# A pooling branch's projection as Strassen products over output pairs, feature halves and token halves

## The chip, the cores and the metric

The kernel runs on one core of one Trainium2 chip. The metric is the device time of one execution in microseconds, as a median of several runs. All matrix products are float32 products made of three matmuls on float32r pieces (high part times high part, high times low, low times high), so one logical 128x128 by 128x512 product is three TensorE instructions.

## The reference, cut to what matters

One layer of a hybrid decoder trunk, with 1024 tokens of 1024 channels. The part that the change touches is the product `y_a W_a` in the middle of this:

```python
h = rms_norm(x, norm_mix)
u_pool, q, k, v, g_a, g_b = split(h @ w_in)
y_a = pool_mixer(u_pool, w_pool, pool_scale)      # 1024 tokens x 512 channels
y_b = stick_breaking_attention(q, k, v)           # 8 heads of 64
merged = sigmoid(g_a) * (y_a @ w_branch_a) + sigmoid(g_b) * (y_b @ w_branch_b)
x = x + merged @ w_out                            # then SwiGLU, embedding gate, norm
```

`w_branch_a` is 512 x 1024.

## The kernel before

Everything is kept transposed: a tile has 128 channels on the partitions and 512 tokens (half of the sequence, `HALF`) on the free axis. Stages that follow one another and matter here:

- The stage of `u`, then four projections to q and k (`to_qk`, 0, 4, 1, 5) with the four pooling groups (`pool_mix`) between them. `pool_mix` makes window sums on VectorE in tiles `win`, splits them into `plh` and `pll`, multiplies by `w_pool` (two halves of three matmuls) and evicts with `split_gain` straight into float32r pairs `yah`, `yal` of 128 x 1024 (one ScalarE and one VectorE instruction for each half).
- The projection to v: 8 banks of PSUM `vb`, 192 matmuls with the weights moving. Bank `tt` holds 128 tokens; it is evicted in four instructions, ScalarE and VectorE in turn (`split_gain` on even and odd heads), into a tile `vs` of 4 KB a partition, of which there are two, and then written to `d_v` in HBM. Token tiles 0, 2, 4, 6 use the first `vs`, and 1, 3, 5, 7 the second. A `vs` is free again when its write has landed.
- The projection of the pooling branch, which is what changes: for each of eight output blocks `m` a weight load of 128 x 512 (`w_a[m]`), its split into `whi` and `wlo`, and for each half of the tokens a bank of PSUM that gathers four channel blocks of three matmuls each (`project`, lines 84 to 86), 192 matmuls in all. ScalarE copies the bank into a tile `ev` or `sg` (two of each), and that is written to `d_t[m]` in HBM. Behind the weight of `m == 2` the loads of head 0 of the attention (`head_loads(0)`, tiles `hq`, `hkh`, `hkl`, `hv`) are issued.
- The attention, with an order of TensorE's instructions that is written out by hand. The remaining projections to q and k and the two gates run in it as fillers; `gate_a` reads `d_t` back.

Outside the parts written out by hand a planner lays the instructions of each engine in an order: of those that it takes to be ready, the one earliest in the program. The order in the queue of an engine is then fixed, and an engine waits at the front of its queue.

SBUF is handed out as two stacks of pools, one growing from the left and one (`side="right"`) from the right. A pool that is opened after another has been closed lies over the closed one's bytes, and a tile there waits for the old tiles with which it shares bytes, and for those alone (`reuse_waits="tile"`). In a pool, the tiles of one name lie side by side, the names in order of their first use, and the first tile of a name takes the lowest place. In KB a partition, from where `up` begins: `up` has `u0` to `u3` (16); `ab` has `wpraw`, `wph`, `wpl`, `evh`, `evl` (2 each), `win`, `plh`, `pll` and `vs` (two of 4 each). When these are closed, `hlp` (two each of `hq`, `hkh`, `hkl`, `hv`, 4 each) and then the pool of the attention (`beta`, `fail` two of 4 each, `evh`, `evl` two of 2 each, then `ath` of 2 each) begin at the same byte. `wp` holds two each of `wraw`, `whi`, `wlo` (4 each).

Of the kernel before, what the change touches and what calls it, by code (L numbers as in the profile page):

```python
# [25 lines left out]
HALF = 512  # L26
# [18 lines left out]
def hybrid_block(ctx, tc, xT, pT, gains, pscale, w_u, w_qk, w_v, w_ga, w_gb, w_pool, w_a, w_b,  # L45
                 w_out, w_gate, w_up, w_down, w_pg, w_pp, out):
    nc = tc.nc

    def pool(name, bufs=1, **kw):
        return tc.tile_pool(name=name, bufs=bufs, reuse_waits="tile", **kw)  # L50
# [11 lines left out]
    ps_sb = const.tile([P, 4], F32, name="ps_sb")  # L62
# [5 lines left out]
    def hs(h):  # L68
        return slice(h * HALF, (h + 1) * HALF)


    def weight(src, cols):
        raw = wp.tile([P, D], F32, name="wraw")
        hi = wp.tile([P, D], F32R, name="whi")
        lo = wp.tile([P, D], F32R, name="wlo")
        nc.sync.dma_start(raw[:, :cols], src)
        for c in range(0, cols, HALF):
            cs = slice(c, c + HALF)
            split(hi[:, cs], lo[:, cs], raw[:, cs])
        return hi, lo  # L80

    def mm3(ps, w, x, first, last, onto=False):

        nc.tensor.matmul(ps, w[0], x[0], start=first, stop=False, skip_group_check=onto)  # L84
        nc.tensor.matmul(ps, w[0], x[1], start=False, stop=False, skip_group_check=onto)  # L85
        nc.tensor.matmul(ps, w[1], x[0], start=False, stop=last, skip_group_check=onto)  # L86

    def col(w, k):
        return w[0][:, k * P:(k + 1) * P], w[1][:, k * P:(k + 1) * P]

    def part(x, sl):
        return x[0][:, sl], x[1][:, sl]

    def steps(ps, w, x, sl, n=KT):
        for k in range(n):
            mm3(ps, col(w, k), part(x[k], sl), k == 0, k == n - 1)
            yield

    def project(ps, w, x, sl, n=KT):
        for _ in steps(ps, w, x, sl, n):  # L100
            pass

    def split(hi, lo, src, eng=None):
# [42 lines left out]
    def new_pair():  # L146
        return xhp.tile([P, S], F32R, name="xs"), xhp.tile([P, S], F32R, name="xs")
# [10 lines left out]
    d_t = [scr(f"d_t{i}", [P, S]) for i in range(KT)]  # L158
# [11 lines left out]
    wp = ph1.enter_context(pool("wp", 2))  # L170
    tmp = ph1.enter_context(pool("tmp", 2))
    xhx = ph1.enter_context(ExitStack())
    xhp = xhx.enter_context(pool("xhp", 2 * KT))
    ab = ph1.enter_context(ExitStack())
    up = ab.enter_context(pool("up"))
    ps8x = ph1.enter_context(ExitStack())
    ps8 = ps8x.enter_context(pool("ps8", 8, space=PSUM))
# [5 lines left out]
    with pool("start") as st:  # L183
        acc = st.tile([P, S], F32, name="acc")
        ps = ps8.tile([P, HALF], F32, name="mm")
# [3 lines left out]
        for k in range(KT):  # L189
            xt = st.tile([P, S], F32, name="xt", bufs=3)  # L190
            w = st.tile([P, HALF], F32, name="wraw", bufs=3)
            wh = st.tile([P, HALF], F32R, name=f"wuh{k}")
            wl = st.tile([P, HALF], F32R, name=f"wul{k}")
            pair = new_pair()
# [66 lines left out]
            move(dst[0, :, hs(h)], hi)  # L261
            move(dst[1, :, hs(h)], lo)

    yap = ExitStack()
    yp = yap.enter_context(pool("yap", side="right"))
    abp = ab.enter_context(pool("ab"))

    ya = []
    raw = abp.tile([P, 4 * P], F32, name="wpraw")
    wph = abp.tile([P, 4 * P], F32R, name="wph")  # L270
    wpl = abp.tile([P, 4 * P], F32R, name="wpl")
    nc.sync.dma_start(raw, w_pool)
    split(wph, wpl, raw)

    def pool_mix(g, w):
        cur, step = u[g], 1
        while step < w:
            nxt = abp.tile([P, S], F32, name="win", bufs=2)
            nc.vector.tensor_add(nxt[:, :S - step], cur[:, :S - step], cur[:, step:])
            nc.vector.tensor_copy(nxt[:, S - step:], cur[:, S - step:])  # L280
            cur, step = nxt, step * 2
        po = abp.tile([P, S], F32, name="win", bufs=2)
        n = S - w + 1
        nc.vector.scalar_tensor_tensor(po[:, :n], cur[:, :n], 1.0 / w, u[g][:, :n], ALU.mult, ALU.subtract)
        nc.vector.tensor_mul(po[:, n:], cur[:, n:], rcnt[:, 16 - w:15])
        nc.vector.tensor_sub(po[:, n:], po[:, n:], u[g][:, n:])
        pl = (abp.tile([P, S], F32R, name="plh", bufs=2), abp.tile([P, S], F32R, name="pll", bufs=2))
        split(*pl, po)
        y = (yp.tile([P, S], F32R, name=f"yah{g}"), yp.tile([P, S], F32R, name=f"yal{g}"))
        for h in range(2):  # L290
            ps = ps8.tile([P, HALF], F32, name="mm")
            mm3(ps, col((wph, wpl), g), part(pl, hs(h)), True, True)
            split_gain(*part(y, hs(h)), ps, ps_sb[:, g:g + 1])
        ya.append(y)

    def run(x):
        for _ in x:
            pass
# [6 lines left out]
    pool_mix(2, WINDOWS[2])  # L305
    run(to_qk(abp, ps8, 5))
    pool_mix(3, WINDOWS[3])


    vb = [ps8.tile([P, HALF], F32, name="mm") for _ in range(KT)]  # L310
    for j in range(4):
        w = weight(w_v[j], D)
        for e in range(2):
            k = 2 * j + e
# [54 lines left out]
        return q, kh, kl, v  # L369

    loads = {}
    for m in range(KT):
        w = weight(w_a[m], 4 * P)
        if m == 2:
            loads[0] = head_loads(0)
        for h in range(2):
            ps = ps8.tile([P, HALF], F32, name="mm")
            project(ps, w, ya, hs(h), 4)
            t = tmp.tile([P, HALF], F32, name=("ev", "sg")[h])
            nc.scalar.copy(t, ps)  # L380
            nc.sync.dma_start(d_t[m][:, hs(h)], t)
    ps8x.close()
    yap.close()

# [5 lines left out]
    with att, pool("att", 2) as ap, ExitStack() as pss:  # L390
# [111 lines left out]
        with tc.manual_schedule(engines={nc.tensor.engine}):  # L502
            for s in range(len(slots) + LAG + AVLAG):
                if s < len(slots):
                    h, qt = slots[s]
# [20 lines left out]
    def bank():  # L526
        return psp.tile([P, HALF], F32, name="mm")
# [3 lines left out]
    for i, t in enumerate(yb):  # L531
        pair = ybsp.tile([P, S], F32R, name=f"ybh{i}"), ybsp.tile([P, S], F32R, name=f"ybl{i}")
# [44 lines left out]
    for m in range(KT):  # L577
        w = weight(w_b[m], 4 * P)
        for h in range(2):
            sg = rp.tile([P, HALF], F32, name="rg")  # L580
# [3 lines left out]
            ps = bank()  # L584
# [32 lines left out]
    for m in range(KT):  # L617
        w = pieces(w_out[m])
        nc.sync.dma_start(x2[m][:, hs(0)], xT[m][:, hs(0)])
        ps = bank()  # L620
# [7 lines left out]
    for m in range(4):  # L628
        w = pieces(w_out[m])
        nc.sync.dma_start(x2[m][:, hs(1)], xT[m][:, hs(1)])  # L630
        ps = bank()
        whole(ps, w, mg, hs(1))
        if m == 3:
            w = pieces(w_out[4])
# [150 lines left out]
    for m in range(4, KT):  # L785
        ps = bank()
# [3 lines left out]
        if m < KT - 1:  # L790
            w = [halves(r) for r in raws]
# [21 lines left out]
    y = const.tile([P, KT], F32, name="nrm_y", bufs=2)[:, :4]  # L813
# [24 lines left out]
    y12 = normed(0, 1)  # L838
    for i in range(4):
        y22 = normed(i + 4, 1)  # L840
        nc.scalar.copy(b22[i][0], y22)
        nc.gpsimd.tensor_sub(unsplit[i][1], y22, y12)
        y11 = normed(i, 0)
        if i < 3:
            embed(i + 1, 0)
        nxt = normed(i + 1, 1) if i < 3 else None
# [25 lines left out]
        y12 = nxt  # L872
# [209 lines left out]
    pair = [Weights(0, 0), Weights(0, 1)]  # L1082
# [3 lines left out]
    for m2 in range(KT // 2):  # L1086
        w = plain_w[m2] if m2 < 2 else halves(plain_weights(m2))
        if m2 > 1:
            pair[m2 - 2].sums()
        for e in range(2):  # L1090
            for h in range(2):
                ps = bank()
# [18 lines left out]
    with tc.manual_schedule(engines={e.engine for e in (nc.tensor, nc.vector, nc.scalar, nc.gpsimd, nc.sync)}):  # L1111
# [9 lines left out]
        for u, (c, mpp) in enumerate(units):  # L1121
            if mpp == 0:
                nxt = {}
# [16 lines left out]
            for slot in range(14):  # L1140
                n, i = divmod(slot, 2)
                for w, e in loads.get(slot, ()):
                    w.load(e)
                w, cols = pair[i].w[n]
                name = "xzxyxyx"[n]
                x = op[DOWN[n]] + ([last[DOWN[n]]] if c == NC - 1 else [])
                ps = banks[i][name] = product(w, x, cols, banks[i].get(name))
# [12 lines left out]
            pair = ahead  # L1160
# [45 lines left out]
    for m in range(KT):  # L1206
        w = pieces(w_pg[m])
# [22 lines left out]
    ws = []  # L1230
    for m in range(KT):
        w = pieces(w_pg[m])
# [25 lines left out]
    ps = spread(psp, dg, 2)  # L1258
# [50 lines left out]
```

## Time and profile before

| | us |
|---|---|
| median of 3 runs | 1452.06 |
| lowest and highest | 1450.31, 1454.25 |
| the profiled execution | 1453.29 |
| its span | 1451.6 |

The profile is of one execution; its times count from the span's start. PE is the row of TensorE's matmuls, DVE VectorE, ACT ScalarE, POOL GpSimd and SP the queue that issues DMAs. The end of a matmul is modelled and overlaps the next one's start, so the pace of TensorE is the distance of two starts, not the duration of one.

### The profile page before, as it was taken

The numbers are of one execution on the slowest core, as the hardware profiler recorded it, in microseconds if no ns is written. First come the engines' busy times: TensorE is split into PE (matmuls) and PEld (weight loads), VectorE is DVE, ScalarE is ACT, GpSimd is POOL, SyncE is SP. The second block draws the span as 40 slices with busy tenths as digits, with TensorE's granted clock in tenths as the row PEclk, the third lists the DMA queues.
The fourth block names the chain that finished last, engine by engine and source line by source line (L and its number), as shares of the span: only waits on it lengthen the run. The fifth ranks groups of instructions, "written<-read, shape, count | busy, mean of one in ns | idle before, by whom it ended". The sixth has DMA issues, their size and how long they took to land.

```text
span 1451.6 us, 19083 instructions
## 1 busy us (share of the span) xinstructions
PE 1419.4 (98%) x6546; PEld 1169.5 (81%) x6546; DVE 1003.4 (69%) x1595; ACT 626.8 (43%) x1174; POOL 352.8 (24%) x435
## 2 busy tenths in 40 slices
PE   9999999999999999999899999999999999999995
PEld 7888888888888878887688888888888788888785
DVE  6671268888877876577756666666664877789786
ACT  6131455555555543345544444444443222226453
POOL 0000012333223300002324434444443433320002
PEclk9999999999999999999999999999999999999998
DMA  7140875455443167434234444444439566622352
GB/s 227 48 140 22 276 217 160 137 152 153 133 118 93 59 206 258 134 106 145 73 116 150 148 152 152 153 160 159 146 141 335 176 237 242 261 73 91 111 180 69
DMA packets 100657, 221.74 MB, mean 153 GB/s; under 512 B 10704, under 2 KB 22480, under 8 KB 100560
## 3 DMA queue, kind: packets, MB, share of 16 engines
q1 hardware_dynamic: 100560, 220.52, 45.7%
q8 instruction: 52, 0.85, 0.3%
q14 instruction: 45, 0.37, 0.1%
HBM read 151.80 MB, written 68.68 MB: 152 GB/s over the span
## 4 chain that ended last, share of the span: by engine, by line
PE 81%; issue 8%; DVE 7%; POOL 2%; ACT 1%; DMA 1%; POOLq 0%; DVEq 0%; SPq 0%; ACTq 0%
PE mm L86 25%; PE mm L84 25%; PE mm L85 25%; DVE fail L418 1%; PE pt L436 1%; PE av L452 1%; PE av L451 1%; DVE wlo L105 1%; PE z L408 1%; PE z L409 1%; PE mm L117 1%; PE mm L143 0%; POOL fail L416 0%; DVE ev L614 0%; PE mm L217 0%
## 5 line engine op out<-in xcount | busy, mean ns | idle before, releaser
L84 PE MATMUL mm<-t,whi 128*128 128x512 f32 x896 | 353.5, 395 | 7.1 <-ACT whi L104 5.5
L104 ACT CAST whi<-wraw 128x512 fp32r<-128x512 f32 x316 | 192.8, 620 | 378.1 <-PE mm L85 238.0
L86 PE MATMUL mm<-t,wlo 128*128 128x512 f32 x896 | 352.7, 394 | 0.9 <-DVE wlo L105 0.8
L85 PE MATMUL mm<-t,whi 128*128 128x512 f32 x896 | 351.9, 393 | 0.0
L105 DVE TENSOR_TENSOR wlo<-wraw,whi 128x512 fp32r<-128x512 f32 x316 | 226.1, 722 | 135.7 <-ACT whi L104 134.9
L84 PEld LDWEIGHTS mm<-t,whi 128*128 128x128 f32 x896 | 168.6, 188 | 47.9 <-ACT whi L104 6.7
L86 PEld LDWEIGHTS mm<-t,wlo 128*128 128x128 f32 x896 | 168.5, 188 | 41.2 <-DVE wlo L105 2.9
L85 PEld LDWEIGHTS mm<-t,whi 128*128 128x128 f32 x896 | 168.7, 188 | 38.0 <-issue 0.2
L84 PE MATMUL mm<-xs,whi 128*128 128x512 f32 x384 | 154.6, 403 | 0.0
L86 PE MATMUL mm<-xs,wlo 128*128 128x512 f32 x384 | 150.3, 391 | 0.0
L85 PE MATMUL mm<-xs,whi 128*128 128x512 f32 x384 | 150.2, 391 | 0.0
L1117 DVE TENSOR_TENSOR x<-mm,x 128x512 f32<-128x512 f32 x140 | 96.4, 690 | 42.7 <-PE mm L86 38.9
L418 DVE TENSOR_TENSOR_SCAN fail<-fail 128x1024 f32<-128x1024 f32 (+3 forms) x64 | 87.3, 1364 | 27.4 <-POOL fail L416 27.0
L685 POOL TENSOR_TENSOR ws<-wraw 128x512 f32<-128x512 f32 x22 | 30.2, 1373 | 302.2 <-DMA wraw<-in_w_gate 209.2
L105 DVE TENSOR_TENSOR t<-ev,t 128x512 fp32r<-128x512 f32 x79 | 74.0, 954 | 34.9 <-ACT t L104 34.6
L104 ACT CAST ath<-pt 128x256 fp32r<-128x256 f32 (+1 forms) x176 | 54.8, 335 | 69.7 <-PE pt L436 39.3
L86 PEld LDWEIGHTS mm<-xs,wlo 128*128 128x128 f32 x384 | 72.1, 188 | 15.8
L104 ACT CAST t<-ev 128x512 fp32r<-128x512 f32 x79 | 48.1, 620 | 78.2 <-DVE ev L761 41.3
L84 PEld LDWEIGHTS mm<-xs,whi 128*128 128x128 f32 x384 | 72.2, 188 | 11.8 <-ACT sg L380 0.2
L85 PEld LDWEIGHTS mm<-xs,whi 128*128 128x128 f32 x384 | 72.3, 188 | 11.5
L416 POOL TENSOR_SCALAR_AFFINE_SELECT fail<-fail 128x128 f32<-128x128 f32 x64 | 20.7, 323 | 226.4 <-ACT fail L414 203.3
L105 DVE TENSOR_TENSOR atl<-pt,ath 128x256 fp32r<-128x256 f32 (+1 forms) x176 | 61.4, 367 | 18.1 <-ACT ath L104 17.8
(227 smaller groups left out, 2602.3 us busy)
## 6 DMA issues: line engine op xcount, KB each, us to landing
d_t<-t SPq DMA_DIRECT2D x36, 512.0 KB, 3.3
t<-d_t SPq DMA_DIRECT2D x36, 512.0 KB, 6.7
d_b<-t SPq DMA_DIRECT2D x27, 512.0 KB, 2.6
t<-d_b SPq DMA_DIRECT2D x27, 512.0 KB, 6.7
wraw<-in_w_gate SPq DMA_DIRECT2D x44, 256.0 KB, 2.8
wraw<-in_w_up SPq DMA_DIRECT2D x44, 256.0 KB, 3.1
wraw<-in_w_down SPq DMA_DIRECT2D x44, 256.0 KB, 4.5
wraw<-in_w_out SPq DMA_DIRECT2D x32, 256.0 KB, 3.0
```

The lines of the kernel that those rows point to most:

```text
L84: nc.tensor.matmul(ps, w[0], x[0], start=first, stop=False, skip_group_check=onto)
L85: nc.tensor.matmul(ps, w[0], x[1], start=False, stop=False, skip_group_check=onto)
L86: nc.tensor.matmul(ps, w[1], x[0], start=False, stop=last, skip_group_check=onto)
L104: nc.scalar.copy(hi, src)
L105: (eng or nc.vector).tensor_sub(lo, src, hi)
L117: nc.tensor.matmul(ps[:, t:t + 1], a[:, t * P:(t + 1) * P], ones[:, :1], start=i == 0, stop=i == len(accs) - 1)
L408: nc.tensor.matmul(zo, q[:, base:base + P], kh[:, ks], start=True, stop=False)
L409: nc.tensor.matmul(zo, q[:, base:base + P], kl[:, ks], start=False, stop=True)
L416: nc.gpsimd.affine_select(r[:, :P], r[:, :P], [[1, P]], ALU.is_gt, 1.0, base=0, channel_multiplier=-1)
L418: nc.vector.tensor_tensor_scan(r[:, :w], r[:, :w], r[:, :w], 1.0, ALU.mult, ALU.bypass)
L685: nc.gpsimd.tensor_add(a["s1"], a["a21"], a["a22"])
L1117: nc.vector.tensor_add(xx, ps, xx)
```

## The change

`pool_mix` evicts its products with one scaled copy on ScalarE into float32 halves `ya{g}{h}` of 128 x 512 in a pool of their own (`yf`). Its work tiles move into a pool `mix` that closes behind the fourth group. Then come seven operands for each of two channel blocks `i` (28 tiles of 128 x 512 in the right-hand pool `yap`): three of them are halves as they are, four are sums formed in place; each is split into a float32r pair. These instructions stand in the program ahead of the projection to v.

The projection runs over four pairs of output blocks. A pair's two weight loads go into one `wraw`; quarters 0, 1 and 3 are split into `whi`, `wlo`; four VectorE sums form the other weights in place; the sums are split into `wsh`, `wsl` of a new pool `wap` (two of each, opened behind `hlp`). Seven products of six matmuls each follow, 168 matmuls in all, in three banks of PSUM of which `x` takes p1, p6, p7 and p4 one after another and `y` p5 and p3. Between products a bank's content is copied out by ScalarE or added by VectorE.

```diff
-    yap = ExitStack()
-    yp = yap.enter_context(pool("yap", side="right"))
-    abp = ab.enter_context(pool("ab"))
+    yfp = ab.enter_context(pool("yf"))
+    abp = ab.enter_context(pool("abp"))
+    mix = ExitStack()
+    mixp = mix.enter_context(pool("mix"))
...
-        y = (yp.tile([P, S], F32R, name=f"yah{g}"), yp.tile([P, S], F32R, name=f"yal{g}"))
+        y = [yfp.tile([P, HALF], F32, name=f"ya{g}{h}") for h in range(2)]
         for h in range(2):
             ps = ps8.tile([P, HALF], F32, name="mm")
             mm3(ps, col((wph, wpl), g), part(pl, hs(h)), True, True)
-            split_gain(*part(y, hs(h)), ps, ps_sb[:, g:g + 1])
+            nc.scalar.activation(y[h], ps, AF.Copy, scale=ps_sb[:, g:g + 1])
...
+    mix.close()
+    yap = ExitStack()
+    yp = yap.enter_context(pool("yap", side="right"))
+    wa = {n: [] for n in ("p1", "p2", "p6", "p5", "p7", "p3", "p4")}
+
+    def operand_a(n, i, y):
+        pair = tuple(yp.tile([P, HALF], F32R, name=f"{n}{i}{c}") for c in "hl")
+        split(*pair, y)
+        wa[n].append(pair)
+
+    for i in range(2):
+        (y11, y12), (y21, y22) = ya[i], ya[i + 2]
+        operand_a("p1", i, y11)
+        operand_a("p2", i, y21)
+        operand_a("p3", i, y22)
+        nc.vector.tensor_sub(y11, y12, y11)
+        operand_a("p5", i, y11)
+        nc.vector.tensor_sub(y12, y22, y12)
+        operand_a("p7", i, y12)
+        nc.vector.tensor_sub(y22, y22, y11)
+        operand_a("p6", i, y22)
+        nc.vector.tensor_sub(y21, y21, y22)
+        operand_a("p4", i, y21)
...
-    for m in range(KT):
-        w = weight(w_a[m], 4 * P)
-        if m == 2:
-            loads[0] = head_loads(0)
-        for h in range(2):
-            ps = ps8.tile([P, HALF], F32, name="mm")
-            project(ps, w, ya, hs(h), 4)
-            t = tmp.tile([P, HALF], F32, name=("ev", "sg")[h])
-            nc.scalar.copy(t, ps)
-            nc.sync.dma_start(d_t[m][:, hs(h)], t)
+    wax = ExitStack()
+    wap = wax.enter_context(pool("wap", 2))
+    Q = 2 * P
...
+    def product_a(w, n, i, ps=None):
+        first = ps is None
+        ps = ps8.tile([P, HALF], F32, name="mm") if first else ps
+        for k in range(2):
+            x = wa[n][k]
+            mm3(ps, col((quarter(w[0], i), quarter(w[1], i)), k), x, first and k == 0, k == 1, not first)
+        return ps
...
+    for mp in range(KT // 2):
+        raw = wp.tile([P, D], F32, name="wraw")
+        for e in range(2):
+            nc.sync.dma_start(raw[:, hs(e)], w_a[2 * mp + e])
+        w = tuple(wp.tile([P, D], F32R, name=n) for n in ("whi", "wlo"))
+        ws = tuple(wap.tile([P, D], F32R, name=n) for n in ("wsh", "wsl"))
+        split(w[0][:, hs(0)], w[1][:, hs(0)], raw[:, hs(0)])
+        split(quarter(w[0], 3), quarter(w[1], 3), quarter(raw, 3))
+        a11, a12, a21, a22 = (quarter(raw, i) for i in range(4))
+        nc.vector.tensor_add(a22, a21, a22)
+        nc.vector.tensor_sub(a21, a11, a21)
+        nc.vector.tensor_sub(a11, a22, a11)
+        nc.vector.tensor_sub(a12, a12, a11)
+        if mp == 1:
+            loads[0] = head_loads(0)
+        x = product_a(w, "p1", 0)
+        c11 = kept_a(x, "ev")
+        ps = product_a(w, "p2", 1)
+        nc.vector.tensor_add(c11, ps, c11)
+        put(c11, 2 * mp, 0)
+        for c in range(2):
+            split(ws[0][:, hs(c)], ws[1][:, hs(c)], raw[:, hs(c)])
+        product_a(ws, "p6", 0, x)
+        c12 = kept_a(x, "sg")
+        y = product_a(ws, "p5", 3)
+        c22 = kept_a(y, "ev")
+        product_a(ws, "p7", 2, x)
+        nc.vector.tensor_add(c22, x, c22)
+        put(c22, 2 * mp + 1, 1)
+        product_a(ws, "p3", 1, y)
+        nc.vector.tensor_add(c12, y, c12)
+        put(c12, 2 * mp, 1)
+        product_a(w, "p4", 3, x)
+        put(kept_a(x, "sg"), 2 * mp + 1, 0)
+    wax.close()
```

`kept_a` copies a bank on ScalarE into a tile of `tmp`, and `put` writes such a tile to `d_t`.

## Rows read from the trace of the kernel before

**Rows 1.** The page's busy times by engine.

```profile
PE 1419.4 (98%) x6546; PEld 1169.5 (81%) x6546; DVE 1003.4 (69%) x1595; ACT 626.8 (43%) x1174; POOL 352.8 (24%) x435
```

**Rows 2.** Busy by stage: window, its us, then engines, PEclk, DMA share, GB/s.

```profile
54.69:103.65 48.96, 48.96 (x217) 40.54 (x216) 42.41 (x68) 16.22 (x26) 0.00 (x0) 1.00 0.30 108
103.65:147.17 43.52, 43.52 (x193) 36.04 (x192) 7.79 (x14) 6.14 (x12) 0.00 (x0) 1.00 0.20 59
147.17:191.96 44.79, 44.79 (x193) 36.03 (x192) 11.57 (x21) 18.60 (x36) 0.35 (x2) 1.00 0.83 267
```

**Rows 3.** Groups by form, 147.17 to 191.96: line, shapes, xcount | busy, mean ns | idle.

```profile
L84 PE MATMUL mm<-yah,whi 128*128 128x512 f32 x64 | 25.3, 395 | 0.0
...
L105 DVE TENSOR_TENSOR wlo<-wraw,whi 128x512 fp32r<-128x512 f32 x9 | 6.1, 691 | 30.7 <-ACT whi L104 30.7
L109 DVE SCALAR_TENSOR_TENSOR vs<-mm,icol,vs 128x256 fp32r<-128x256 f32 x12 | 5.5, 481 | 3.9 <-ACT vs L108 3.9
L104 ACT CAST whi<-wraw 128x512 fp32r<-128x512 f32 x9 | 5.5, 620 | 14.3 <-PE mm L85 8.6 <-PE mm L86 2.6 <-DMA wraw<-in_w_qk 2.4
L108 ACT ACTIVATE vs<-mm,icol 128x256 fp32r<-128x256 f32 x12 | 5.4, 474 | 2.1 <-DVE vs L109 1.9
L380 ACT COPY ev<-mm 128x512 f32<-128x512 f32 x8 | 4.7, 586 | 10.0 <-PE mm L86 4.3 <-DMA d_t<-ev 3.7 <-issue 1.9
```

**Rows 4.** PE in time, the stage's first matmul and the one behind its last.

```profile
147.17 0.40 PE L84 MATMUL mm<-yah,whi 128*128 128x512 f32 x1
...
191.96 0.39 PE L408 MATMUL z<-hkh,hq 128*128 128x512 f32 x1
```

**Rows 5.** Groups by form: evictions and splits of the pooling, and a 256-wide add.

```profile
L109 DVE SCALAR_TENSOR_TENSOR yal<-mm,ps_sb,yah 128x512 fp32r<-128x512 f32 x8 | 5.5, 744 | 0.0
...
L105 DVE TENSOR_TENSOR evl<-ev,evh 128x512 fp32r<-128x512 f32 x8 | 5.5, 687 | 0.7 <-ACT evh L104 0.7
...
L607 DVE TENSOR_TENSOR acc<-acc,ev 128x256 f32<-128x256 f32 x4 | 1.7, 423 | 1.4 <-ACT ev L606 1.4
```

**Rows 6.** SP in time, 143 to 167: issues of the writes of v.

```profile
144.71 0.96 SPq L151 DMA_DIRECT2D d_v<-vs  x2
...
150.21 1.78 SPq L151 DMA_DIRECT2D d_v<-vs  x2
...
155.79 1.81 SPq L151 DMA_DIRECT2D d_v<-vs  x2
...
161.62 1.74 SPq L151 DMA_DIRECT2D d_v<-vs  x2
```

**Rows 7.** DMA issues, 144 to 167: xcount, KB each, median us to landing.

```profile
d_v<-vs SPq DMA_DIRECT2D x8, 512.0 KB, 2.7
```

**Rows 8.** POOL in time: a tile of the attention's pool, and its wait.

```profile
165.92 0.21 POOL L426 MEMSET ath<- 128x128 f32 x1 [164.09 <-DMA d_v<-vs]
```

**Rows 9.** PE in time, 703.5 to 713: a stand of PE and the pace behind it.

```profile
703.86 0.39 PE L86 MATMUL mm<-t,wlo 128*128 128x512 f32 x1
709.46 0.79 PE L84 MATMUL mm<-t,whi 128*128 128x512 f32 x1 [5.21 <-ACT whi L104]
...
710.91 0.63 PE L84 MATMUL mm<-t,whi 128*128 128x512 f32 x1
711.33 0.63 PE L85 MATMUL mm<-t,whi 128*128 128x512 f32 x1
...
712.50 0.40 PE L85 MATMUL mm<-t,whi 128*128 128x512 f32 x1
```

**Rows 10.** Busy by window, behind two stands of PE: the granted clock.

```profile
709.40:712.20 2.80, 2.74 (x7) 2.04 (x8) 2.77 (x5) 0.64 (x2) 0.00 (x0) 0.50 0.25 86
...
1355.40:1361.00 5.60, 5.60 (x14) 4.43 (x15) 3.87 (x17) 0.42 (x1) 0.00 (x0) 0.51 0.16 49
```

**Rows 11.** PE's waits, 695 to 715: us in total, times, longest.

```profile
PE mm L84 <- ACT ev L700: 1.5, 1, 1.5
```

**Rows 12.** ACT in time: a copy that waits for its tile's write.

```profile
179.90 0.59 ACT L380 COPY ev<-mm 128x512 f32<-128x512 f32 x1 [3.66 <-DMA d_t<-ev]
```

More of the change, by code (lines that the diff above doesn't have):

```diff
@@ L262, in to_qk @@
             move(dst[1, :, hs(h)], lo)
-    yap = ExitStack()
-    yp = yap.enter_context(pool("yap", side="right"))
-    abp = ab.enter_context(pool("ab"))
+    yfp = ab.enter_context(pool("yf"))
+    abp = ab.enter_context(pool("abp"))
+    mix = ExitStack()
+    mixp = mix.enter_context(pool("mix"))
     ya = []
-    raw = abp.tile([P, 4 * P], F32, name="wpraw")
-    wph = abp.tile([P, 4 * P], F32R, name="wph")
-    wpl = abp.tile([P, 4 * P], F32R, name="wpl")
+    raw = mixp.tile([P, 4 * P], F32, name="wpraw")
+    wph = mixp.tile([P, 4 * P], F32R, name="wph")
+    wpl = mixp.tile([P, 4 * P], F32R, name="wpl")
     nc.sync.dma_start(raw, w_pool)
@@ L277, in pool_mix @@
         while step < w:
-            nxt = abp.tile([P, S], F32, name="win", bufs=2)
+            nxt = mixp.tile([P, S], F32, name="win", bufs=2)
             nc.vector.tensor_add(nxt[:, :S - step], cur[:, :S - step], cur[:, step:])
@@ L281, in pool_mix @@
             cur, step = nxt, step * 2
-        po = abp.tile([P, S], F32, name="win", bufs=2)
+        po = mixp.tile([P, S], F32, name="win", bufs=2)
         n = S - w + 1
@@ L286, in pool_mix @@
         nc.vector.tensor_sub(po[:, n:], po[:, n:], u[g][:, n:])
-        pl = (abp.tile([P, S], F32R, name="plh", bufs=2), abp.tile([P, S], F32R, name="pll", bufs=2))
+        pl = (mixp.tile([P, S], F32R, name="plh", bufs=2), mixp.tile([P, S], F32R, name="pll", bufs=2))
         split(*pl, po)
-        y = (yp.tile([P, S], F32R, name=f"yah{g}"), yp.tile([P, S], F32R, name=f"yal{g}"))
+        y = [yfp.tile([P, HALF], F32, name=f"ya{g}{h}") for h in range(2)]
         for h in range(2):
@@ L371, in hybrid_block, with quarter @@
     loads = {}
-    for m in range(KT):
-        w = weight(w_a[m], 4 * P)
-        if m == 2:
-            loads[0] = head_loads(0)
-        for h in range(2):
-            ps = ps8.tile([P, HALF], F32, name="mm")
-            project(ps, w, ya, hs(h), 4)
-            t = tmp.tile([P, HALF], F32, name=("ev", "sg")[h])
-            nc.scalar.copy(t, ps)
-            nc.sync.dma_start(d_t[m][:, hs(h)], t)
+    wax = ExitStack()
+    wap = wax.enter_context(pool("wap", 2))
+    Q = 2 * P
+    def quarter(t, i):
+        return t[:, i * Q:(i + 1) * Q]
@@ new lines, in product_a, with put, kept_a @@
+    def product_a(w, n, i, ps=None):
[5 more added lines that the diff above has]
+        return ps
+    def put(t, m, h):
+        nc.sync.dma_start(d_t[m][:, hs(h)], t)
+    def kept_a(ps, name):
+        t = tmp.tile([P, HALF], F32, name=name)
+        nc.scalar.copy(t, ps)
+        return t
```

## The prediction

> **What bounds the kernel now.** The page first: PE is busy 98% of the span [rows 1], so a stage is worth reading by PE's pace. The busy times by stage [rows 2] come next: while v is computed (103.65 to 147.17) and in the pooling branch's projection (147.17 to 191.96) PE is busy all the time at full clock, and DVE and ACT have most of it free. The groups of the second stretch say the same: no matmul group has idle time before it [rows 3]. So the projection takes what its matmuls take: 191.96 - 147.17 = 44.79 us [rows 4] for 192 matmuls, 0.2333 us from start to start. The reader should then look at what else happens in that stretch, as PE's row doesn't show it: the eviction of v is not over when the projection begins. Its writes are issued in pairs, and the last of the eight goes out at 161.62 + 1.74 - 0.32 (the length of one issue) = 163.04 [rows 6], lands some 2.7 us later [rows 7], and a tile of the attention's pool that shares bytes with `vs` waits until 165.92 for it [rows 8]. In the kernel before nobody on PE cares.
>
> **The change part by part.** *Matmuls.* 4 pairs x 7 products x 6 = 168 instead of 192: 24 x 0.2333 = 5.6 us less PE work. By the Trainium skill, "TensorE: Matmul & The Clock Gate", Part 1, a 512-column matmul starts every 215.7 ns at full clock; the sum would be 5.2 us by it, this stage shows 233.3 ns, and the row is taken.
>
> *Pooling's eviction and the operands.* Eight DVE instructions of 0.744 us go [rows 5]. The operands add 14 splits and 8 subtractions: 22 x 0.687 = 15.1 us on DVE [rows 5] and 14 x 0.62 = 8.7 us on ACT [rows 3]. They can start when the last pooling group is evicted, near 103.65; the right-hand pool of 56 KB reaches over `win`, `plh` and `pll`, free at the same time. From there to 147.17 DVE has 43.52 - 7.79 = 35.7 us free and ACT 37.4 [rows 2]. Cost nothing; without that cover the first products would wait up to 15 us.
>
> *Weights.* The same eight loads and sixteen writes. For a pair, ACT: splits 0.62 + 0.62 + 0.62 and one quarter (at most 0.62), four copies of 0.586, at most 4.8 us; DVE: three splits of 0.69 and one quarter and four sums at 0.42, three adds of 0.69, 6.2 us [rows 3, 5]. A pair has 42 x 0.2333 = 9.8 us of matmuls, so neither engine becomes the bound.
>
> *The memory of `wsh` and `wsl`.* Here the change adds a wait. Counted from where `up` begins, in KB a partition: after the change `up` has 0 to 16, `yf` 16 to 32 (eight halves of 2), `abp` has `evh` 32 to 34, `evl` 34 to 36, and the two `vs` at 36 to 40 and 40 to 44. When they close, `hlp` takes 0 to 32, and `wap` begins at 32: `wsh` at 32 and 36, `wsl` at 40 and 44. So the first `wsl`, which pair 0 uses, lies exactly on the second `vs`, that of token tiles 1, 3, 5, 7, and can't be written before the last write of v has landed. The same arithmetic can be tried on the kernel before: there the second `vs` lies at 54 to 58, and the attention's first `ath` at 32 + 8 + 8 + 4 + 4 = 56, and that tile does wait for `d_v<-vs` [rows 8], although later places of its name were free. p6, the third product, needs `wsl`. Behind it on PE's queue everything waits, except what the planner has put ahead: p1 and p2 of pair 1, which need only `whi` and `wlo` (free when v ends), are ready then, and I take them as put ahead. Nothing more can run: p5, p7 and p3 need `wsl` too, p4 adds into p7's bank, and pair 2's weights wait for p4 of pair 0.
>
> When does the last write of v land? Second-`vs` issues lie at 144.71 + 0.96 - 0.32 = 145.35, then 151.67, 157.28 and 163.04: 6.3, 5.6 and 5.8 us apart [rows 6]. At least it is the landing (2.7) and four instructions in turn (2 x 0.474 + 2 x 0.481 = 1.9) with some 0.4 for five hand-overs, 5.0 us [rows 3, 7]. The weight splits and copies that stood between them become fewer, so I take 6.0 + 5.3 + 5.3: 161.95, landing at 164.7. `wsl`'s subtraction (0.69) and the hand-overs: p6 starts at 165.7. PE stops at 147.17 + 24 x 0.2333 = 152.8, and stands for 12.9 us.
>
> By the Trainium skill, "Perfetto Trace Analysis", Optimization Strategy, a recurring gap on the engine that should be saturated can mean that there isn't enough SBUF for the next tile; the POOL row agrees that a tile can wait for another stage's bytes, and without that wait the sum would be the 5.6 us gain.
>
> *The clock.* Behind a stand of 5.21 us, 7 matmuls started 0.43 us apart at 0.50 granted (1.2 of 2.4 GHz) [rows 9, 10]: 7 x 0.2 = 1.4 us lost. Behind another, 14 ran at 0.51 [rows 10]: 2.8. I take 2.0.
>
> *The banks.* Before, each product had a bank of eight; now a bank is reused after one product, 1.40 us. From a last matmul's start: its end 0.39, the copy 0.59 or the add 0.69, hand-overs: 1.1 us against 1.40 + 0.23. 0.5 is left, which one other instruction ahead in the queue (0.62) uses up, and a copy can wait for its tile's write, as one did for 3.66 us [rows 12]. The nearest row is one reuse that cost PE 1.5 us [rows 11]. Between 0 and 3 us over 16 such turns; I take 0.7, nearer to none, as both engines are half idle.
>
> *The rest.* The head loads, seven DMAs, go behind pair 1's weights, in about the same place; z needs them some 10 us later than before. The attention's first bank may wait for the last copy, up to 1 us; taken as none, as before.
>
> *Sum.* -5.6 + 12.9 + 2.0 + 0.7 = +10.0 us. The profiled execution took 1453.29 (span 1451.6); its sum is 1463.3. The median of the runs is 1.2 lower, so 1462.1.
>
> **The rivals.** *A. PE keeps the order of the program.* p1 and p2 of pair 1 stay behind p6; PE stands from 150.0, 2.8 us more: +12.8, 1464.9. For it: no row shows PE taking matmuls out of the program's order; against it: the planner puts the first ready one next, and DVE's order is mixed. *B. The wait isn't there.* Not slower: the tiles land elsewhere than I count, or the planner gives pair 0 the other place of `wsl`, at 44 to 48, which only `mix` has used. It decides by those 4 KB alone. The gain is then 5.6 us less what the banks cost while ACT and DVE also evict v: 1446.5 with nothing lost, some 1449 with 2.5 lost, no more than 1452 with 5.6. Against it: in each pool of two the first tile takes the lower place. *C. The writes of v come sooner or later.* At 5.0 us a turn p6 starts at 164.1: +7; as before, with 165.92 and a subtraction, at 167: +11.3. *D. The change doesn't do what it says*: the planner pulls the operands past v's end; the first products wait, up to 15 us, on top.
>
> **How the numbers follow.** Forecast with C's bounds 0.57, A 0.20, B 0.18, D 0.05. Low end of the forecast: p6 at 164.1, 144 matmuls at the pace of the v stage (43.52/192 = 0.2267), clock 1.4, no loss at banks: 164.1 + 32.6 + 1.4 - 191.96 = +6.2, or 1458.2; high end: A with p6 at 167, clock 2.8 and banks 3: +12.8 + 1.3 + 0.8 + 2.3 = +17.2, or 1469.3. The range 1457 to 1469 holds nearly all but B and part of D. About 0.3%, 4.4 us, is what a measurement of this kernel tells from no change. B splits into 0.08 faster by more, 0.10 within; of the forecast, 0.03 may come under 4.4. So faster 0.08, same 0.13, slower 0.79.
>
> **What would show it.** Right: one stand of PE of 11 to 16 us between 150 and 168, ended by the subtraction into `wsl`, whose wait is a DMA `d_v<-vs`; clock 0.50 behind it; 168 matmuls at 0.233 else; `z` starting near 202; v's stretch without idle PE. Wrong: `wsl` written before 150; PE's gaps short and spread over all pairs (then the banks are the bound); or p1 waiting at 147.

## The result, and the profile after

| | before | after |
|---|---|---|
| median, us | 1451.87 (1450.31 to 1454.25, 4 runs) | 1463.93 (1463.16 to 1465.44, 4 runs) |
| the profiled execution, us | 1453.29 | 1463.16 |
| its span, us | 1451.6 | 1461.5 |
| the projection of the pooling branch, first matmul to `z`, us | 44.79 [rows 4] | 56.27 |

The kernel became slower: after / before is 1.0084, 95% interval 1.0071 to 1.0098. It runs 24 matmuls fewer and needs 12 us more.

The page's busy times by engine, of after:

```profile
PE 1416.6 (97%) x6522; PEld 1167.0 (80%) x6522; DVE 1028.5 (70%) x1645; ACT 638.4 (44%) x1196; POOL 354.9 (24%) x435
```

Beside [rows 1]: 24 matmuls less and 2.8 us less of PE's busy time, though 24 x 0.2333 are 5.6; the rest shows that some matmuls took longer. DVE got 25.1 us more, ACT 11.6. Where the time lies is seen by stage. A stand is a time in which PE stops and waits. The windows of after (us, then PE, PEld, DVE, ACT and POOL busy, granted clock, DMA share, GB/s): v and the projection; and then the projection cut into its first stand, the two matmuls behind it with the second stand, the stretch at half clock, and the rest.

```profile
103.65:147.17 43.52, 43.52 (x194) 36.04 (x193) 21.04 (x37) 13.93 (x28) 0.00 (x0) 1.00 0.54 145
146.33:202.60 56.27, 42.46 (x169) 33.49 (x168) 27.83 (x52) 22.16 (x43) 0.41 (x2) 0.85 0.54 193
153.00:160.80 7.80, 0.00 (x0) 0.00 (x0) 3.73 (x8) 3.75 (x10) 0.00 (x0) 0.50 0.55 221
160.80:164.30 3.50, 1.22 (x2) 0.50 (x2) 0.72 (x2) 1.64 (x3) 0.00 (x0) 0.50 0.56 227
164.30:169.60 5.30, 5.28 (x13) 4.15 (x14) 1.77 (x3) 1.17 (x2) 0.00 (x0) 0.50 0.94 267
169.60:202.60 33.00, 33.00 (x143) 26.77 (x142) 16.85 (x29) 11.96 (x22) 0.41 (x2) 1.00 0.49 172
```

Set the first two against [rows 2]: while v is computed PE is still busy all the time at full clock, although DVE now does 21.0 us of work there instead of 7.8 and ACT 13.9 instead of 6.1. The operands cost nothing. All of the loss is in the second window, and there in its first 23 us: from 169.60 on PE never stops.

PE's waits in that stretch (us in total, times, longest), and PE in time around them:

```profile
PE mm L84 <- ACT wsh L104: 11.6, 1, 11.6
PE mm L86 <- DVE wsl L105: 2.3, 1, 2.3
```

```profile
148.89 0.40 PE L86 MATMUL mm<-p21h,wlo 128*128 128x512 f32 x1
160.84 0.80 PE L84 MATMUL mm<-p60h,wsh 128*128 128x512 f32 x1 [11.55 <-ACT wsh L104]
161.43 0.63 PE L85 MATMUL mm<-p60l,wsh 128*128 128x512 f32 x1
164.32 0.80 PE L86 MATMUL mm<-p60h,wsl 128*128 128x512 f32 x1 [2.26 <-DVE wsl L105]
...
169.60 0.40 PE L86 MATMUL mm<-p70h,wsl 128*128 128x512 f32 x1
...
202.60 0.39 PE L483 MATMUL z<-hkh,hq 128*128 128x512 f32 x1
```

The reader should see two stands, not one. p6 of the first pair waits first for `wsh`, at 160.84, runs two matmuls, and waits then for `wsl`, at 164.32. By distances of starts the stands are 160.84 - 148.89 - 0.23 = 11.7 us and 164.32 - 161.43 - 0.43 = 2.5 us, 14.2 in all. Then 12 starts fill the 5.28 us to 169.60, 0.43 us apart but for the first (0.60) and the last (0.41), and from 169.60 the pace is back. ACT and DVE show what each stand waited for; the first line of DVE is the last of the first pair's four sums:

```profile
159.81 0.47 ACT L108 ACTIVATE vs<-mm,icol 128x256 fp32r<-128x256 f32 x1 [0.55 <-DVE vs L109]
160.18 1.12 ACT L104 CAST wsh<-wraw 128x512 fp32r<-128x512 f32 x2
```

```profile
138.79 0.43 DVE L434 TENSOR_TENSOR wraw<-wraw 128x256 f32<-128x256 f32 x1
...
163.58 2.50 DVE L105 TENSOR_TENSOR wsl<-wraw,wsh 128x512 fp32r<-128x512 f32 x4 [2.78 <-DMA d_v<-vs]
```

The first pair's copies into `wsh` have no wait of their own, and what they read was ready at 139.2, some 21 us before. They stand on ACT's queue right behind the last of v's evictions. The subtraction into `wsl` does have a wait, 2.78 us, for a write of v.

### The profile page after: what moved, and what is told of

The parts are those of the page before. It is cut to its first block, busy times and chain, and to the rows that moved or that the text cites. A ratio compares the mean times of both kernels' runs of the same rounds, so it can differ in the third digit from the quotient of the medians.

```text
span 1461.5 us, 19116 instructions
## 1 busy us (share of the span) xinstructions
PE 1416.6 (97%) x6522; PEld 1167.0 (80%) x6522; DVE 1028.5 (70%) x1645; ACT 638.4 (44%) x1196; POOL 354.9 (24%) x435
## 4 chain that ended last, share of the span: by engine, by line
PE 78%; issue 8%; DVE 8%; ACT 2%; POOL 2%; DMA 2%; SPq 0%; POOLq 0%; DVEq 0%; ACTq 0%
PE mm L86 24%; PE mm L85 24%; PE mm L84 24%; DVE fail L493 1%; PE pt L511 1%; DVE wlo L105 1%; DVE ev L689 1%; PE av L527 1%; PE av L526 1%; PE z L483 1%; PE z L484 1%; PE mm L117 1%; DMA d_v<-vs 1%; ACT whi L104 0%; POOL fail L491 0%
## 5 line engine op out<-in xcount | busy, mean ns | idle before, releaser
L84 PEld LDWEIGHTS mm<-xs,whi 128*128 128x128 f32 x384 | 72.3, 188 | 12.1 <-ACT sg L418 0.5
L85 PEld LDWEIGHTS mm<-xs,whi 128*128 128x128 f32 x384 | 72.4, 189 | 11.5
L492 POOL TENSOR_SCALAR_AFFINE_SELECT beta<-beta 128x128 f32<-128x128 f32 x64 | 66.7, 1042 | 23.1 <-ACT beta L490 22.1
```

Source lines behind the costliest of these rows:

```text
L492: nc.gpsimd.affine_select(b[:, :P], b[:, :P], [[1, P]], ALU.is_gt, 0.0, base=0, channel_multiplier=-1)
```

## The experiments

All are edits of the kernel after. None leaves anything out. "Stage" is from the first matmul of p1 to `z`. Each ratio is against the kernel before, run beside it on the same chip; its median there lay between 1452.0 and 1452.4. The interval of after itself, 1.0071 to 1.0098, overlaps those of e3, e4, e6 and e10, so their small differences from after are read from the stage of the profiled execution, and the medians only stand beside it.

### What the stand hangs on: PE's order, the clock, bytes or pools

**e3, p1 and p2 of the second pair put ahead of p6 by hand.** In the loop over pairs, everything up to the split into `wsh` becomes `head_a`, the rest `tail_a`:

```diff
+    first = head_a(0)
+    second = head_a(1)
+    tail_a(0, *first)
+    tail_a(1, *second)
+    for mp in range(2, KT // 2):
+        tail_a(mp, *head_a(mp))
```

> The changed kernel with p1 and p2 of pair 1 written ahead of p6 of pair 0 in the program, as the forecast had taken the planner to place them; all else stays, the wait too. Theory (the stand ends when the eviction of v lets it, whatever PE does before): 12 matmuls, 2.8 us, move into the stand, which ends where it did (160.8 and 164.3); 1461, 2.5 to 2.8 us under the changed kernel. Rival (the later products of pair 0 or the banks hold the end, so that nothing is gained): 1463 to 1465.

1461.61 us, ratio 1.0065 (1.005 to 1.008). PE in time, at p1, at the two stands, and at `z`:

```profile
151.06 0.50 PE L84 MATMUL mm<-p10h,whi 128*128 128x512 f32 x1 [0.60 <-DVE vs L109]
...
162.55 0.80 PE L84 MATMUL mm<-p60h,wsh 128*128 128x512 f32 x1 [8.44 <-ACT wsh L104]
...
166.03 0.80 PE L86 MATMUL mm<-p60h,wsl 128*128 128x512 f32 x1 [2.25 <-DVE wsl L105]
...
202.45 0.50 PE L493 MATMUL z<-hkh,hq 128*128 128x512 f32 x1 [1.00 <-ACT sg L418]
```

The first stand is 3.1 us shorter (8.44 for 11.55), but p1 of the second pair now waits 0.6 us for a bank that still holds v, and `z` waits 1.0 us for the last copy. The stage (147.50 to 202.45) is 54.95 us, 1.3 less than in after; the medians differ by 2.3. So the order of PE on which the forecast and its rival A differed is worth some 1 to 2 us, and no more; the stand doesn't end sooner, 15.0 us behind the first matmul of p1 for 14.5 in after.

**e6, the first stand filled with matmuls whose result nobody reads.**

```diff
+        if mp == 0:
+            idle = ps8.tile([P, HALF], F32, name="mm")
+            for j in range(40):
+                nc.tensor.matmul(idle, w[0][:, :P], wa["p1"][0][0], start=True, stop=True)
```

> The changed kernel with 40 matmuls of 512 columns into a bank that nobody reads, in front of p6 of pair 0: 9.3 us of idle work in the stand of 11.7, so that TensorE isn't idle before p6. They add nothing to the path if they fit. Measures the term of the clock by itself. Theory: the granted clock stays 1.00 through p6 and p5, the 2.8 us that 15 matmuls at 0.43 us lose against 0.233 come back, less what the filler pushes p6 back (0 to 1.5 us): 1461 to 1463. If the clock had no part in the loss: unchanged, or later by as much as the filler overruns.

1462.67 us, ratio 1.0074 (1.0057 to 1.0091). Windows: the fillers, the first two matmuls of p6, and the stretch behind the second stand; then PE in time at the two stands that are left.

```profile
150.50:160.00 9.50, 9.47 (x40) 7.45 (x40) 4.97 (x12) 3.68 (x8) 0.00 (x0) 1.00 0.62 248
161.00:163.00 2.00, 0.73 (x2) 0.30 (x2) 0.37 (x1) 1.19 (x3) 0.00 (x0) 1.00 0.93 375
165.00:168.00 3.00, 3.00 (x7) 2.40 (x8) 1.64 (x3) 0.59 (x1) 0.00 (x0) 0.50 0.86 252
```

```profile
161.41 0.50 PE L84 MATMUL mm<-p60h,wsh 128*128 128x512 f32 x1 [1.34 <-ACT wsh L104]
...
164.89 0.80 PE L86 MATMUL mm<-p60h,wsl 128*128 128x512 f32 x1 [2.75 <-DVE wsl L105]
```

With the fillers the clock is still granted in full when p6 starts, which is as expected, but it doesn't stay so through p6 and p5: behind the second stand, 2.75 us after two matmuls, it is at half, and 7 starts lie 0.42 to 0.6 us apart, where after had 12 behind that stand and 2 ahead of it. Of the 3 us that the clock costs in after (worked out below) the stage shows 56.27 - 55.31 = 1.0 back; the medians differ by 1.3. The clock term is real, but this filler buys back only a third of it, as a second stand follows.

**e4, the first pair's `wsh` and `wsl` placed where no tile `vs` has a byte.** Four tiles of one buffer, in an order that puts only the second pair's on `vs`:

```diff
-    wap = wax.enter_context(pool("wap", 2))
+    wap = wax.enter_context(pool("wap"))
+    wst = {n: wap.tile([P, D], F32R, name=n) for n in ("wsh0", "wsh1", "wsl1", "wsl0")}
...
-        ws = tuple(wap.tile([P, D], F32R, name=n) for n in ("wsh", "wsl"))
+        ws = wst[f"wsh{mp % 2}"], wst[f"wsl{mp % 2}"]
```

> The changed kernel with the four tiles of wsh and wsl laid out so that pair 0's share no byte with vs: wsh over evh and evl, wsl over the mixing pool, and pair 1's two over the two vs. The pool is the same. Tells the bytes from the pool. If a tile waits only for the bytes it shares, as the prediction had it: p6 of pair 0 runs at 149 without a stand, pair 1's waits from 159 to near 164, some 4 to 5 us of stand in all, and the time is 1452 to 1455. If the planner holds the whole new pool behind the whole old one (wsh's copies and wsl's subtractions then stand in ACT's and DVE's queues behind all of v's eviction): p6 of pair 0 starts at 160.8 as before, only its third matmul comes sooner, at 162 instead of 164.3: 1461 to 1462.

1461.5 us, ratio 1.006 (1.0045 to 1.0075). PE, then ACT and DVE in time:

```profile
162.64 0.80 PE L84 MATMUL mm<-p60h,wsh 128*128 128x512 f32 x1 [11.55 <-ACT wsh L104]
```

```profile
161.60 0.47 ACT L108 ACTIVATE vs<-mm,icol 128x256 fp32r<-128x256 f32 x1 [0.55 <-DVE vs L109]
161.98 1.13 ACT L104 CAST wsh<-wraw 128x512 fp32r<-128x512 f32 x2
...
162.62 1.29 DVE L105 TENSOR_TENSOR wsl<-wraw,wsh 128x512 fp32r<-128x512 f32 x2
165.37 1.29 DVE L105 TENSOR_TENSOR wsl<-wraw,wsh 128x512 fp32r<-128x512 f32 x2 [1.46 <-DMA d_v<-vs]
```

The second stand is gone, and the stage (148.12 to 201.40) is 3.0 us shorter than in after: the first pair's `wsl` no longer waits for a write, and the second pair's does. So that wait goes by bytes, as the prediction had it. The first stand is as long as ever, 11.55 us. The copy into `wsh` shares no byte with `vs` here, as it didn't in after, and is laid on ACT's queue behind all sixteen evictions of v all the same. So there are two things: the wait of a tile goes by its own bytes; the place in the queue, which the planner fixes beforehand, behaves as if the whole new pool had to stay behind the old pool that it overlaps. The expectation that went by bytes alone falls.

### What is next when the stand is shortened or removed

**e2, a third `vs`**, in its old pool, so that v is evicted sooner:

```diff
-        vs = abp.tile([P, H, 2, HD], F32R, name="vs", bufs=2)
+        vs = abp.tile([P, H, 2, HD], F32R, name="vs", bufs=3)
```

> The changed kernel with three tiles vs instead of two, in the same pool, so wsh and wsl still lie over that pool. Theory (p6 of pair 0 waits until the eviction of v is through): the eviction takes some 1.8 us a token tile instead of 2.4 and ends near 157 instead of 160.8 to 164, p6's six matmuls run from near 157, the stand is shorter by 4 to 6 us, and the time is 1458 to 1460. If it were the memory of wsl alone (it now shares bytes with the tiles of tokens 2 and 5, written by 155), p6 would start near 155.5. Rival (the stand has another cause than the eviction of v): 1463 to 1465, unchanged.

1457.95 us, ratio 1.0033 (1.0024 to 1.0042).

```profile
157.01 0.80 PE L84 MATMUL mm<-p60h,wsh 128*128 128x512 f32 x1 [6.81 <-ACT wsh L104]
```

The eviction of v has to wait for its own writes less often, and p6 starts 3.8 us sooner with it, though p1 starts 0.9 later (147.24). The stand follows the eviction of v, and the stage is 48.8 us (147.24 to 196.02).

**e1, `vs` in a pool of its own beneath `yf`**, so that `wap` lies on other pools and `hlp` on `vs`; **e5**, the same with three `vs`:

```diff
+    vsp = ab.enter_context(pool("vsp"))
     yfp = ab.enter_context(pool("yf"))
...
-        vs = abp.tile([P, H, 2, HD], F32R, name="vs", bufs=2)
+        vs = vsp.tile([P, H, 2, HD], F32R, name="vs", bufs=2)
```

> One line moves: the two tiles vs get a pool of their own below the pool of the pooling halves, so that wsh and wsl lie over those halves, evh, evl and the mixing pool, and hkl (head 0 of the attention) lies over vs. The sums and all else stay. Theory (the loss is the wait of the pair-0 weights for the eviction of v, through the memory that they share): PE goes on from p2 to p6 of pair 0 without a stand, 168 matmuls at 0.233 us take 39.2 us from 146.3 or 147.2, z starts near 186, and the time is the 5.6 us below the kernel before that the matmuls save, plus what the banks cost while v is evicted, 0 to 3 us: 1446 to 1449. Rival (the banks: a bank reused after 1.40 us is what makes the change slow, the stand is only where it shows first): gaps of PE between the products of all pairs, the time stays above 1455. Rival (operands or splits are late on ACT and DVE, whatever the memory): p6 of pair 0 still waits for wsh, 1460 or more.

> As the run with vs in its own pool, with three tiles vs instead of two, so that the eviction of v waits less for its writes and leaves ACT and DVE sooner. Theory: PE has no stand in either, so 0 to 1.5 us less than with two, by what the eviction of v takes from the bank turns of pairs 0 and 1: 1445 to 1448. Rival (the banks bound the stage at every pair): no change against two tiles, both above 1455.

e1: 1454.1 us, ratio 1.0012 (1.0004 to 1.0021); e5: 1452.94, ratio 1.0004 (0.9995 to 1.0013). Both miss what was expected by about 5 us. p6 no longer stands, as expected, but the stage is 47.05 us in e1, where 168 matmuls at pace are 39.2. e1 in time: PE, the copy that PE waits for, and SP's queue before it; then the window behind the stand.

```profile
181.06 0.80 PE L84 MATMUL mm<-p70h,wsh 128*128 128x512 f32 x1 [3.90 <-ACT sg L419]
...
188.74 0.50 PE L84 MATMUL mm<-p70h,wsh 128*128 128x512 f32 x1 [0.81 <-ACT sg L419]
```

```profile
180.43 0.59 ACT L419 COPY sg<-mm 128x512 f32<-128x512 f32 x1 [8.01 <-DMA d_t<-sg]
```

```profile
165.85 0.52 SPq L151 DMA_DIRECT2D hq<-d_q  x1
...
170.23 0.59 SPq L151 DMA_DIRECT2D hv<-d_v  x1
171.07 1.45 SPq L415 DMA_DIRECT2D d_t<-sg  x2
```

```profile
181.00:186.30 5.30, 5.24 (x12) 4.09 (x13) 2.08 (x3) 0.60 (x2) 0.00 (x0) 0.50 0.70 240
```

This is a new wait in the place of the removed one. p7 needs the bank that a copy into `sg` must empty, and that copy waits 8.0 us for the earlier write of the same tile. The write was issued behind the loads of a head, which in e1 go out only behind the writes of v, from 165.85 on, in the middle of the projection. In after all but those of `hv` had gone out at 104 to 132, beside v. In e1 `hkl` lies on `vs`, but `hq` lies on `up` alone and the profile shows no wait of its loads; they are late all the same. So the place in SP's queue, too, goes with the overlap of the pools. Stands of 3.9 and 0.8 us, and 2.5 of low clock (12 starts in the 5.29 us from 181.06 to 186.35), are 7.2 of the 7.9 us above pace. In e5 the waits are smaller and more (2.2, 0.6, 0.4, 0.4 and 0.3 us), and the stage is 46.2 us.

### Neither on `vs`

**e7, `vs` above a wider `abp`, and one each of `wsh` and `wsl`.** `wap` then lies on `evh` and `evl`, `hlp` on `up` and `yf`, and nothing on `vs` that the projection or the head's loads use:

```diff
-    abp = ab.enter_context(pool("abp"))
+    abp = ab.enter_context(pool("abp", 2))
+    vsp = ab.enter_context(pool("vsp"))
...
-        vs = abp.tile([P, H, 2, HD], F32R, name="vs", bufs=2)
+        vs = vsp.tile([P, H, 2, HD], F32R, name="vs", bufs=2)
...
-    wap = wax.enter_context(pool("wap", 2))
+    wap = wax.enter_context(pool("wap"))
```

> The changed kernel with vs above evh and evl (two of each) in a pool of its own, and with one wsh and one wsl instead of two, so that neither wap (over evh, evl) nor hlp (over up and yf) lies over vs. Against the run with vs below the pooling halves it differs in one thing that matters: hlp is free early, and the fourteen loads of hq, hkh and hkl for heads 0 and 1 go out before v is through, as in the changed kernel, instead of at 165.9 in the middle of the projection. Theory (what was left in that run, 3.9 and 0.8 us of stand and the low clock behind it, is a copy that waits for its tile sg, whose write queued behind those loads): no stand over 1 us between 147 and 187, z at 186 to 187.5, 1446 to 1448. Rival (the banks themselves: ACT and DVE late while v is evicted, or single wsh and wsl late at each pair): stands at p6 or p7 of each pair, 1450 to 1454.

1446.34 us, ratio 0.9958 (0.9945 to 0.9972): faster than both kernels, by 6.1 us than before and 17.6 than after. The stage, and the first load of a head:

```profile
145.93:185.12 39.19, 39.19 (x170) 31.54 (x168) 25.66 (x50) 20.44 (x41) 0.41 (x2) 1.00 0.76 264
```

```profile
104.14 0.51 SPq L151 DMA_DIRECT2D hq<-d_q  x1
```

168 x 0.2333 = 39.19: no stand, no low clock, no loss at the banks, although `wsh` and `wsl` have one buffer each.

**e9, e1 with one each of `wsh` and `wsl`** (and `abp` as in e7): `wsh` and `wsl` are as in e7, and the head's loads, whose pool lies on `vs` as in e1, are late again.

```diff
+    vsp = ab.enter_context(pool("vsp"))
     yfp = ab.enter_context(pool("yf"))
-    abp = ab.enter_context(pool("abp"))
+    abp = ab.enter_context(pool("abp", 2))
...
-    wap = wax.enter_context(pool("wap", 2))
+    wap = wax.enter_context(pool("wap"))
```

> As the run with all apart (one wsh, one wsl, two evh and evl), but with vs below the pooling halves, so that hlp lies over vs again and the loads of heads 0 and 1 go out when v is through, in the middle of the projection. Between the run with vs below and two wsh, and the run with all apart, this parts the head loads from the number of wsh. Theory (the loads' place is what cost 7 us): an ACT copy into sg or ev waits 2 us or more for its write between 170 and 185, PE stands 2 to 5 us there and runs at the low clock behind it; 1450 to 1454. Rival (the two wsh, and the order of products that the planner makes of them, were the cost): no stand, 1446 to 1448.

1448.82 us, ratio 0.9972 (0.9962 to 0.9982), stage 41.7.

```profile
182.57 0.50 PE L84 MATMUL mm<-p60h,wsh 128*128 128x512 f32 x1 [1.70 <-ACT ev L419]
...
181.93 1.07 ACT L419 COPY ev<-mm 128x512 f32<-128x512 f32 x2 [4.57 <-DMA d_t<-ev]
```

The place of the head's loads is worth 41.7 - 39.2 = 2.5 us (2.5 in the medians as well, though their intervals overlap by a little), by the same mechanism as in e1: a copy that waits for its tile's write. That lies between what the theory and the rival gave. PE's order isn't quite the same in the two: in e9 the last pair's p5 stands ahead of its p6. The other 5.3 us between e1 and e9 came with the second `wsh` and `wsl` (and the narrower `abp`); in e1 the planner mixes products of two pairs on PE (p6 of a pair between p7 and p4 of the one before). Whether two of each cost by themselves, or only where the head's loads are late, is open. In after and in e10, below, two of each with early loads lose nothing once the stands are over, but there the planner doesn't mix the pairs.

**e10, both `vs` in a right-hand pool beside `yap`, two of each kept; e11, the same with one of each.**

```diff
     yp = yap.enter_context(pool("yap", side="right"))
+    vsp = ab.enter_context(pool("vsp", side="right"))
...
-        vs = abp.tile([P, H, 2, HD], F32R, name="vs", bufs=2)
+        vs = vsp.tile([P, H, 2, HD], F32R, name="vs", bufs=2)
```

and in e11 also `pool("wap")` for `pool("wap", 2)`.

> Both vs go to a pool of their own on the right-hand side, above yap, and wap keeps two of each name. So wsh and wsl lie over the byte ranges of abp and mix only, and the head's tiles over up and yf only: nothing that the projection needs and none of the head loads shares a byte with vs. Against e7 it differs in having two wsh and two wsl instead of one; against e1 in that the head loads may go out early. What is still open of e1 (1454.1, where e9 with one of each gave 1448.8): Theory 1, two of each cost by themselves (the planner then has products of two pairs to mix): the stage is then some 44 us and the median near 1451. Theory 2, they cost only together with head loads that are issued inside the stage: the products stand in the program's order, the stage is 39.2 us as in e7, and the median 1446 to 1447. In both, no stand of PE before p6 of the first pair.

> e10 with one wsh and one wsl instead of two. The expectation of e10 counted its bytes wrongly: yap takes 50.4 to 106.4 KB, so vs in the right-hand pool below it takes 42.4 to 50.4, and wap with two of each (32 to 48) reaches 5.6 KB into it, though wsh (32 to 40) doesn't. With one of each wap is 32 to 40 and clear of vs. The order of PE is the same in both. Theory, the planner holds the whole of a new pool behind a closed one that it overlaps anywhere: the stand of 11.6 us goes, the stage is 39.2 to 40 us and the median 1446 to 1447, as in e7. Rival, the other side of SBUF or the pool's place in the program made the wsh copy late: the stand stays, 1461.

e10 was meant to settle that question and couldn't: its expectation took `wap` to be clear of `vs`, and 5.6 KB of them overlap, as e11's says. It showed something else: 1461.39 us, ratio 1.0066 (1.0049 to 1.0083), and the first stand as in after. e10, PE and then ACT:

```profile
159.79 0.80 PE L84 MATMUL mm<-p60h,wsh 128*128 128x512 f32 x1 [11.56 <-ACT wsh L104]
```

```profile
158.76 0.47 ACT L108 ACTIVATE vs<-mm,icol 128x256 fp32r<-128x256 f32 x1 [0.55 <-DVE vs L109]
159.13 2.16 ACT L104 CAST wsh<-wraw 128x512 fp32r<-128x512 f32 x4
```

e11: 1447.84 us, ratio 0.9962 (0.9949 to 0.9974), the first copy into `wsh` and the stage:

```profile
139.31 0.62 ACT L104 CAST wsh<-wraw 128x512 fp32r<-128x512 f32 x1 [1.71 <-DVE wraw L433]
```

```profile
147.31:186.50 39.19, 39.19 (x169) 31.53 (x168) 25.60 (x50) 20.52 (x41) 0.41 (x2) 1.00 0.75 264
```

The stage is as expected, the median 0.8 us above. The two have the same order on PE and differ in one word. With the new pool clear of `vs`, the copies into `wsh` are laid ahead of all of v's evictions, at 139.3 and 140.2, and 16 us of the stage go (55.37 to 39.19). With an overlap of 5.6 KB, at bytes that `wsh` doesn't use, they come at 159.1, behind all of them. That word also changes the number of tiles, from two of each to one, but e1 and e4 tell that apart. In e1, with two of each and `wap` clear of `vs`, the first copy is early as well:

```profile
137.97 0.62 ACT L104 CAST wsh<-wraw 128x512 fp32r<-128x512 f32 x1 [1.71 <-DVE wraw L433]
```

In e4, with one tile of each name and an overlap, it is late. So e4 and e10 are two cases in which the overlap of pools, not of tiles, goes with the copy's place, and `hq` in e1 is a third, on SP. That the planner goes by pools is read from these places; its working was not looked into.

## Why the prediction came out as it did

The forecast of 1462.1 and, in the main, its mechanism, a new pool on the tile that drains v, are borne out: undoing the overlap (e7, e11) takes the whole loss back and gives the gain of the matmuls. How the overlap makes PE wait was only half right, as the list shows. By the Trainium skill, "Perfetto Trace Analysis", Optimization Strategy, a gap that recurs on the saturated engine can mean too little SBUF for the next tile. Here the gap came once, and bytes were not lacking: e1 kept two of each tile, and p6 no longer waited. Where the tiles lay decided.

The terms, in the stage of after (44.79 to 56.27, +11.5):

| term | forecast | measured in after |
|---|---|---|
| 24 matmuls fewer | -5.6 | -5.6 (e7: 39.19 for 44.79) |
| stands of PE | +12.9 | +14.2 (11.7 and 2.5) |
| low clock | +2.0 | +3.0 |
| banks | +0.7 | 0 |
| sum | +10.0 | +11.6 |

The projection also began 0.84 us sooner (146.33 for 147.17), which the forecast didn't have.

- **Operands at no cost: right.** v's stretch has no idle PE. D falls.
- **The wait of `wsl` for v's last write: right**, by bytes, as e4's pair of subtractions shows.
- **p1 and p2 of the second pair put ahead: wrong.** PE kept the program's order, as rival A had it. e3 sizes the step at 1.3 us in the stage and 2.3 in the median. The measured 1463.9 is nearer to A's 1464.9 than to the forecast.
- **When v's last write lands: too late by 1.1 us.** Taken at 164.7; the subtraction started at 163.58. The evictions went round in some 4.8 us a turn: ACT's first eviction of a `vs` came at 152.56 and 157.35 in after. That is even below the 5.0 taken as the least. Rows of before with other work between them were too slow a measure [rows 6]. This error and the one before it partly cancelled: that the sum is nearer than its steps is luck.
- **That only the tile on `vs` waits: wrong.** The text ahead of the prediction says that a tile waits for the tiles whose bytes it shares and for those alone. It holds for the wait, not for the planner's place of an instruction, and the row on which the argument was tried, an `ath` waiting for a write [rows 8], couldn't tell the two apart. The prediction had one stand, ended by `wsl`; there were two, and the first and longer one was ended by `wsh`, which shares no byte with `vs`. It didn't show in the sum, as `wsl` comes last either way. It would have misled a repair: e4 does what the prediction says is enough, and gets 3.0 us of the stage.
- **The clock: mis-sized, 3.0 for 2.0.** The two matmuls between the stands ran at the low clock (0.55 us lost), and 12 starts behind them (5.28 - 12 x 0.2333 = 2.48), a number near the upper end of what [rows 10] gave. That two matmuls between stands would run slow too wasn't foreseen.
- **Banks: 0 for 0.7 in after**, and as small in e7. But the term isn't small by nature. In e1 the same banks cost 4.7 us and the clock behind them 2.5, once the head's loads went out in the stage.
- **The head's loads in about the same place: wrong.** All but those of `hv` moved from the projection (first issue at 165.97 in before) to 104 to 132. In before `hlp` shares no byte with `vs` either, but it reaches into `ab`, the pool that holds `vs`; in after it lies on `up` and `yf` alone. That fits a place by pools, as does `hq` in e1. The text didn't count the move as a gain; e9 against e7 shows that it is worth 2.5 us.
- **Rival B's price**, 1446.5 with nothing lost: e7 measured 1446.3. Its wider end, 1449 to 1452 with losses at the banks, was too kind to e1, which removed the same wait and came to 1454.1.
- **Rival C's +7: a wrong sum.** With p6 at 164.1 in place of 165.7, and all other terms as in the forecast, it is 10.0 - 1.6 = +8.4, still inside the range.

The profiled executions differ by 9.9 us, the medians by 12.1: that of before was 1.4 above its median, that of after 0.8 below.

## What to carry to other kernels

A pool that is opened over a pool still draining by DMA can put the new pool's instructions behind the old one's work in an engine's queue (here ScalarE's, and SP's with the head's loads), even where their tiles share no byte; so lay new pools on tiles that are dead by then, and count the bytes of both pools. Do the same count for prefetched tiles: if their pool lies on the draining tile instead, their loads come out late, in a bunch, ahead of the writes on which the next stage's buffers wait. When a wait is costed, ask what the engine would wait for one step earlier, too.

## What the runs showed of the hardware that was not expected

- Two matmuls between two stands left the granted clock at 0.50 (1.2 of 2.4 GHz): the next 12 starts, 0.43 us apart, were slow as well. When PE had been busy up to 160 (e6), the clock was still full at p6, at 161.41 (1.00), and was at half (0.50) behind a stand of 2.75 us.
- A write of `sg`, 256 KB, landed in a median of 2.2 us in after; in e1 the two that were issued at 171.1 and 172.2 behind the loads of a head took 8.8 and 9.3 us, and the copy started at 180.43. By the Trainium skill, "DMA: Bandwidth & Descriptors", Latency and other measured facts, HBM access takes 0.2 us on average and 2 at high load; the times in e1 are several times that, so most of them would be the transfers queued ahead. No run took them apart.
